# Sparse-attention softmax on negated scores with a running minimum, and a bisection step written as a one-tensor operation

## The chip, the cores and the metric

One Trainium2 chip, one core. The metric is the device time of one execution in microseconds (us), the median of the runs of a kernel. Engines: PE (matmul; PEld is its weight load), DVE (VectorE), ACT (ScalarE), POOL (GpSimd), SP (which issues most transfers).

## The reference

One layer of a streaming encoder over 1,056 rows: 1,024 of a prompt and 32 new rows of a running stream with 128 cached positions. What matters here:

```python
s = einsum('btnd,bld->btnl', qi, ki) * IDX_DIM**-0.5
score = einsum('btnl,btn->btl', relu(s), wi)          # 8 indexer heads
score = where(admissible, score, -inf)
_, idx = top_k(score, k_top)                          # 256 keys (40 for the running stream)
...
logits = einsum('btgrd,btkgd->btgrk', qg, k_sel) * HEAD_DIM**-0.5 + bias
p = softmax(where(valid, logits, NEG))
out = einsum('btgrk,btkgd->btgrd', p, v_sel)          # 8 heads of 64, 2 groups of keys
```

Around it stand one input projection, a gated convolution, the output projection, two layer norms and an MLP of width 4,096 with squared ReLU.

## The kernel before

Activations lie transposed (features on partitions). Products are done in three passes over high and low parts of the operands; the split into these parts is a copy on ACT (line L108) and a subtraction on POOL or DVE (L111). Up to the MLP a scheduler sets the order of the instructions of each engine when the kernel is built, from the program's order and its own estimates; from then on the order is that of the program. Each engine works through its own instructions strictly in the order so fixed.

**Choosing keys (`topk`, L423 on).** Queries are cut into tiles of 128 rows: tile t (0 to 7) sees (t+1)*128 keys; tile 8 is the running stream, with 160. No keys are gathered. For each row, 32 rounds of bisection on the bits of the score find the threshold that 256 keys exceed, and then ties are settled, so that the score tile becomes a mask (0 or a very negative number) which is added to the logits. Tiles 0 and 1 need no choice. A round counts the scores above the candidate, turns the count into a yes or no `v` (L448 or L450) and sets the next candidate `cand` from `v`, `cand` and a bit (L454). Tiles 7 and 6, and later 5, are bisected with `on_act=True`: ACT counts (L441), DVE does L448 and L454 on one element for each partition and tile. Tiles 2, 3, 4 and 8 are done together on DVE: L443 counts, and L450 and L454 handle four columns at a time. All this runs beside the projections, with their DVE evacuations L245, L246, L368, L388 and L414.

**Attention (`att_softmax`, `att_values`).** The tiles come in the order 7, 6, 8, 5, 4, 3, 2, 1, 0 (PLAN), each in four calls (g2 = 0 to 3) of two heads, with pieces of the output projection and of the first layer norm put in between. A call makes the logits on PE (L570 to L574) in one chunk of keys, or in two for tiles 4 to 7; one DVE instruction (L576) for each chunk adds the mask, writes the logits to SBUF and keeps their maximum. Then two small DVE instructions (L580, L581; for one chunk only L583) give the negated maximum `nm` of both heads, ACT takes the exponentials with it as bias and sums them (L586), DVE inverts the two sums (L588), and DVE and ACT scale one head each (L589, L590). PE transposes the weights (L608), ACT and DVE bring them to SBUF in two parts (L615, L616), and PE multiplies them with the values (L624, L625); L629 and L630 bring the result out.

Of the kernel before, what the change touches and what calls it, by code (L numbers as in the profile page):

```python
# [10 lines left out]
F32 = mybir.dt.float32  # L11
# [3 lines left out]
AF = mybir.ActivationFunctionType  # L15
OP = mybir.AluOpType
# [22 lines left out]
LOWEST = -(2.0 ** 126)  # L39
# [25 lines left out]
def f32(ap):  # L65
    return ap.bitcast(F32)
# [3 lines left out]
def hybrid_layer(ctx, tc, xT, win, wkw, wo, w1, w2, ckT, cv, ckiT, scT, cw, lnp, rb, cst, oh,  # L70
                 yT, kT_o, vT_o, kiT_o, pc_o, sc_o):
    nc = tc.nc
    V, S, G, PE = nc.vector, nc.scalar, nc.gpsimd, nc.tensor
# [5 lines left out]
    small = ctx.enter_context(tc.tile_pool(name="small", bufs=3))  # L79
# [20 lines left out]
    def qk_ps():  # L100
        return psum.tile([128, 512], F32, name="qk", bufs=4)

    def tr_ps():
        return psum.tile([128, 512], F32, name="tr", bufs=1)
# [152 lines left out]
    def key_chunks(N):  # L257
        c = (N + 511) // 512
        return [(i * (N // c), N // c) for i in range(c)]
# [34 lines left out]
    ps = tr_ps()  # L294
# [127 lines left out]
    def topk(ts, on_act):  # L422

        nb = len(ts)
        cand = small.tile([128, nb], I32, name="cand")
        cnt = small.tile([128, nb], F32, name="cnt")
        v = small.tile([128, nb], I32, name="v")
        dims = [(score[t], score[t].shape[0], score[t].shape[1], 256 if t < 8 else 40) for t in ts]
        V.memset(cnt, 0.0)

        def junk(R, N):
            return scr.tile([128, 768], F32, name="junka" if on_act else "junk").bitcast(BF16)[:R, :N]

        def scratch(R, n, name):
            return scr.tile([128, 768], F32, name=name)[:R, :n]

        for b in range(31, -1, -1):
            for i, (s, R, N, k) in enumerate(dims):
                c = 0.0 if b == 31 else f32(cand[:R, i:i + 1])
                if on_act:  # L440
                    S.activation(junk(R, N), s, AF.Sign, bias=c, scale=-1.0, accum_out=cnt[:R, i:i + 1])  # L441
                else:
                    V.tensor_scalar(junk(R, N), s, c, -float(k), op0=OP.is_ge, op1=OP.add, accum_out=cnt[:R, i:i + 1])  # L443
            w = -1.0 if b == 31 else float(1 << b)
            for i in (range(nb) if on_act else [slice(None)]):
                vi, ci, ni = (a[:, i:i + 1] if on_act else a for a in (v, cand, cnt))
                if on_act:
                    V.tensor_scalar(vi, ni, float(dims[i][2] - 2 * dims[i][3]), w, op0=OP.is_gt, op1=OP.mult)  # L448
                else:
                    V.tensor_scalar(vi, ni, 0.0, w, op0=OP.is_lt, op1=OP.mult)  # L450
                if b == 31:
                    V.tensor_scalar(ci, vi, 0x40000000, None, op0=OP.bitwise_xor)
                elif b:
                    V.scalar_tensor_tensor(ci, vi, 1 << (b - 1), ci, op0=OP.bitwise_xor, op1=OP.bitwise_xor)  # L454
                else:
                    V.tensor_tensor(ci, vi, ci, op=OP.bitwise_xor)
        if on_act:
            up = small.tile([128, 2, nb], F32, name="up", bufs=1)
            for i, (s, R, N, k) in enumerate(dims):
                th = f32(cand[:R, i:i + 1])  # L460
                V.tensor_scalar(junk(R, N), s, th, -float(k), op0=OP.is_gt, op1=OP.add, accum_out=cnt[:R, i:i + 1])
                for ci, (c, n) in enumerate(key_chunks(N)):
                    e = scratch(R, n, "tie")
                    V.tensor_scalar(e, s[:, c:c + n], th, BIG, op0=OP.is_le, op1=OP.mult)
                    V.tensor_tensor_reduce(e, e, s[:, c:c + n], 1.0, BIG, op0=OP.add, op1=OP.min,
                                           accum_out=up[:R, ci, i:i + 1])
            V.tensor_tensor(up[:, 0], up[:, 0], up[:, 1], op=OP.min)
            V.tensor_scalar(v, cnt, 0.0, -1.0, op0=OP.is_ge, op1=OP.mult)
            x = small.tile([128, nb], I32, name="x", bufs=1)
            V.tensor_tensor(x, cand, up[:, 0].bitcast(I32), op=OP.bitwise_xor)  # L470
            V.tensor_tensor(x, x, v, op=OP.bitwise_and)
            V.tensor_tensor(cand, x, cand, op=OP.bitwise_xor)
        for i, (s, R, N, k) in enumerate(dims):
            th = f32(cand[:R, i:i + 1])
            V.tensor_scalar(junk(R, N), s, th, -float(k), op0=OP.is_gt, op1=OP.add, accum_out=cnt[:R, i:i + 1])
            lim = small.tile([128, 1], F32, name="lim", bufs=1)
            V.tensor_scalar(lim[:R], cnt[:R, i:i + 1], -NEGP, None, op0=OP.mult)
            prev = 0.0
            for c, n in key_chunks(N):
                sc_ = s[:, c:c + n]  # L480
                e, rank = scratch(R, n, "tie"), scratch(R, n, "rank")
                V.tensor_scalar(e, sc_, th, NEGP, op0=OP.is_equal, op1=OP.mult)
                V.tensor_tensor_scan(rank, e, e, prev, op0=OP.add, op1=OP.bypass)
                if c + n < N:
                    carry = small.tile([128, 1], F32, name="carry", bufs=1)
                    V.tensor_copy(carry[:R], rank[:, n - 1:n])
                    prev = carry[:R]
                V.scalar_tensor_tensor(e, rank, lim[:R], e, op0=OP.is_lt, op1=OP.mult)
                V.tensor_scalar(sc_, sc_, th, NEGP, op0=OP.is_lt, op1=OP.mult)
                V.tensor_tensor(sc_, sc_, e, op=OP.add)  # L490

    topk((7, 6), True)
    topk((2, 3, 4, 8), False)
    proj_phase.close()

# [19 lines left out]
    def load_q(t, g):  # L515

        R = 128 if t < 8 else 32
        qs_[t, g] = pb.tile([128, 4, R], F32R, name="q", bufs=3)
        G.dma_start(qs_[t, g], qd[4 * g:4 * g + 4, :, t * 128:t * 128 + R].rearrange("h p t -> p h t"))
# [29 lines left out]
    def att_softmax(t, g2):  # L549

        R, N, k0 = (128, (t + 1) * 128, KP) if t < 8 else (32, 160, 0)
        if g2 % 2 == 0 and (t, g2 // 2) not in qs_:
            load_q(t, g2 // 2)
        q = qs_[t, g2 // 2]
        mask = edge[:R, 256 - N:256] if t < 2 else score[t]
        pad = 128 if t == 0 else 0
        g, h0 = g2 // 2, 2 * (g2 % 2)
        chunks = key_chunks(N)
        mx = small.tile([128, 2, 2], F32, name="mx")
        ls = []  # L560
        for i in range(2):
            L = pb.tile([128, 1024], F32, name="L", tag="L", bufs=LB)[:R, :N]
            ls.append(L)
            qh = q[:, h0 + i, :]
            for ci, (c, n) in enumerate(chunks):
                ps = qk_ps()
                last = ci == len(chunks) - 1
                w = max(n, 256)
                kc = slice(k0 + c - pad, k0 + c - pad + w)
                PE.matmul(ps[:R, :w], qh, kh[g][:, kc], start=True, stop=False)  # L570
                mm = PE.matmul(ps[:R, :w], qh, kl[g][:, kc], start=False, stop=not last)
                if last:
                    PE.matmul(ps[:R, w - 256:w], antir[:, :R], hh[g][:, h0 + i, :], start=False, stop=False)
                    mm = PE.matmul(ps[:R, w - 256:w], antir[:, :R], hl[g][:, h0 + i, :], start=False, stop=True)  # L574
                done["QK"] = mm
                V.tensor_tensor_reduce(L[:, c:c + n], ps[:R, pad:pad + n], mask[:, c:c + n], 1.0, LOWEST,  # L576
                                       op0=OP.add, op1=OP.max, accum_out=mx[:R, ci, i:i + 1])
        nm = small.tile([128, 2], F32, name="nm")
        if len(chunks) == 2:
            V.tensor_tensor(nm[:R], mx[:R, 0], mx[:R, 1], op=OP.max)  # L580
            V.tensor_scalar(nm[:R], nm[:R], -1.0, None, op0=OP.mult)  # L581
        else:
            V.tensor_scalar(nm[:R], mx[:R, 0], -1.0, None, op0=OP.mult)  # L583
        sm = small.tile([128, 2], F32, name="sm")
        for h in range(2):
            S.activation(ls[h], ls[h], AF.Exp, bias=nm[:R, h:h + 1], accum_out=sm[:R, h:h + 1])  # L586
        rs = small.tile([128, 2], F32, name="rs")
        V.reciprocal(rs[:R], sm[:R])  # L588
        V.tensor_scalar(ls[0], ls[0], rs[:R, 0:1], None, op0=OP.mult)  # L589
        S.activation(ls[1], ls[1], AF.Copy, scale=rs[:R, 1:2])  # L590
        return ls
# [736 lines left out]
    n = len(steps)  # L1328
# [124 lines left out]
```

## Time and profile before

| | us |
|---|---|
| median of 3 runs | 1344.34 (1343.89 to 1350.7) |
| the profiled execution's time | 1348.35 |
| its span, first to last instruction | 1346.6 |
| choosing keys beside the projections | about 109 to 362 of the span, tile 5 until 409 |
| attention | about 362 to 575 of the span |

Times are from one profiled execution. A matmul's record can overlap the next one's, so a busy PE isn't PE at its peak. A wait is put down to the instruction that released it.

### The profile page before, as it was taken

How to read it: one execution, taken by the hardware profiler on the slowest of the kernel's cores; microseconds unless marked ns; L12 is line 12 of the kernel's file. 1: busy time of each engine (PE TensorE's matmuls, PEld its weight loads, DVE VectorE, ACT ScalarE, POOL GpSimd, SP SyncE). 2: the span in 40 equal slices, each digit the busy share in tenths (PEclk: the TensorE clock that was granted, in tenths of full speed). 3: DMA queues.
4: the chain of work that ended last, by engine and by line, in shares of the span. 5: the costliest groups of instructions: out<-in, count | busy, mean ns of one | idle time of the engine just before them, and what ended most of it. 6: DMA issues, size and time to landing. Idle time of an engine off the chain costs nothing. (4 is left out here: it accounts for less than half of the span.)

```text
span 1346.6 us, 24097 instructions
## 1 busy us (share of the span) xinstructions
PE 1245.1 (92%) x8822; PEld 1203.5 (89%) x8822; DVE 994.9 (74%) x2043; ACT 692.8 (51%) x1378; POOL 564.6 (42%) x452
## 2 busy tenths in 40 slices
PE   7999999897899988896899999999999999998984
PEld 6999999897788987785899999999999999998884
DVE  5675899999488889878657667666557668586766
ACT  6666988644688878784322222222343444443323
POOL 2412344513521252363453553454445444447632
PEclk9999999899899998988899999999999999998987
DMA  6221111134531221243134343443863663542201
GB/s 209 92 68 37 48 33 47 48 108 152 166 87 18 47 65 32 71 141 122 45 108 150 138 153 139 147 154 137 302 234 91 196 187 113 176 144 87 65 33 65
DMA packets 97222, 149.98 MB, mean 111 GB/s; under 512 B 12456, under 2 KB 41808, under 8 KB 97104
## 3 DMA queue, kind: packets, MB, share of 16 engines
q1 hardware_dynamic: 81664, 139.55, 31.7%
q0 software_dynamic: 9504, 4.33, 1.9%
q10 hardware_dynamic: 5936, 4.58, 1.2%
q8 instruction: 69, 1.13, 0.4%
q14 instruction: 49, 0.40, 0.1%
HBM read 105.41 MB, written 43.00 MB: 110 GB/s over the span
## 5 line engine op out<-in xcount | busy, mean ns | idle before, releaser
L111 POOL TENSOR_TENSOR whl<-wraw,whl 128x512 fp32r<-128x512 f32 (+1 forms) x184 | 251.0, 1369 | 429.6 <-ACT whl L108 408.8
L858 PE MATMUL acc<-b,whl 128*128 128x264 f32 x1088 | 310.9, 286 | 6.1 <-DVE ring L937 3.0
L859 PE MATMUL acc<-b,whl 128*128 128x264 f32 x1088 | 310.7, 286 | 0.0
L860 PE MATMUL acc<-b,whl 128*128 128x264 f32 x1088 | 309.4, 284 | 0.0
L858 PEld LDWEIGHTS acc<-b,whl 128*128 128x128 f32 x1088 | 205.6, 189 | 7.1 <-DVE ring L937 3.2
L860 PEld LDWEIGHTS acc<-b,whl 128*128 128x128 f32 x1088 | 206.1, 189 | 0.0
L859 PEld LDWEIGHTS acc<-b,whl 128*128 128x128 f32 x1088 | 205.1, 189 | 0.1
L108 ACT ACTIVATE whl<-wraw 128x512 fp32r<-128x512 f32 (+1 forms) x184 | 113.1, 623 | 175.3 <-DVE wraw L853 143.2
L131 PE MATMUL mm<-xh,whl 128*128 128x384 f32 (+4 forms) x520 | 172.3, 332 | 14.3 <-ACT whl L108 5.6
L132 PE MATMUL mm<-area,whl 128*128 128x384 f32 (+4 forms) x552 | 182.9, 332 | 0.4 <-DVE area L111 0.4
L133 PE MATMUL mm<-xh,whl 128*128 128x384 f32 (+4 forms) x520 | 169.6, 331 | 0.0
L111 DVE TENSOR_TENSOR b<-xraw,b 128x528 fp32r<-128x528 f32 x94 | 69.7, 742 | 87.1 <-ACT b L108 87.0
L108 ACT ACTIVATE b<-xraw 128x528 fp32r<-128x528 f32 x94 | 60.5, 644 | 136.0 <-PE acc L860 82.1
L441 ACT ACTIVATE junka<-s,cand 128x1024 bf16<-128x1024 f32 (+1 forms) x93 | 96.5, 1037 | 42.0 <-DVE cand L454 34.2
L131 PEld LDWEIGHTS mm<-xh,whl 128*128 128x128 f32 (+1 forms) x520 | 97.9, 188 | 18.1 <-issue 8.1
L132 PEld LDWEIGHTS mm<-area,whl 128*128 128x128 f32 (+1 forms) x552 | 104.5, 189 | 2.9 <-DVE area L111 0.8
L133 PEld LDWEIGHTS mm<-xh,whl 128*128 128x128 f32 (+1 forms) x520 | 97.6, 188 | 3.2 <-POOL whl L111 1.2
L111 POOL TENSOR_TENSOR whl<-at,whl 128x512 fp32r<-128x512 f32 x56 | 81.5, 1465 | 30.8 <-ACT whl L108 30.8
L443 DVE TENSOR_SCALAR_CACHE_REDUCE junk<-s,cand 128x384 bf16<-128x384 f32 (+1 forms) x124 | 80.2, 647 | 1.3
L858 PE MATMUL acc<-area,whl 128*128 128x264 f32 x240 | 69.0, 288 | 0.0
L859 PE MATMUL acc<-area,whl 128*128 128x264 f32 x240 | 68.7, 286 | 0.0
L860 PE MATMUL acc<-area,whl 128*128 128x264 f32 x240 | 68.5, 286 | 0.0
(310 smaller groups left out, 3345.9 us busy)
## 6 DMA issues: line engine op xcount, KB each, us to landing
hd<-ring SPq DMA_DIRECT2D x98, 264.0 KB, 2.1
xraw<-hd SPq DMA_DIRECT2D x98, 264.0 KB, 2.7
at<-in_w_dram SPq DMA_DIRECT2D x58, 256.0 KB, 3.7
wraw<-in_win_dram SPq DMA_DIRECT2D x52, 256.0 KB, 2.6
wraw<-in_wo_dram SPq DMA_DIRECT2D x40, 256.0 KB, 2.7
w_a<-in_w_dram SPq DMA_DIRECT2D x23, 256.0 KB, 3.7
w_c<-in_w_dram SPq DMA_DIRECT2D x19, 256.0 KB, 3.4
zz<-zd SPq DMA_DIRECT2D x4, 1056.0 KB, 8.4
```

Source lines behind the costliest of these rows:

```text
L108: S.activation(hi, raw, AF.Copy)
L111: (lo_eng or G).tensor_tensor(lo, raw, f32(hi), op=OP.subtract)
L131: PE.matmul(ps, wh[k], a, start=(k == 0), stop=False)
L132: PE.matmul(ps, wh[k], b, start=False, stop=False)
L133: PE.matmul(ps, wl[k], a, start=False, stop=(k == K - 1))
L441: S.activation(junk(R, N), s, AF.Sign, bias=c, scale=-1.0, accum_out=cnt[:R, i:i + 1])
L443: V.tensor_scalar(junk(R, N), s, c, -float(k), op0=OP.is_ge, op1=OP.add, accum_out=cnt[:R, i:i + 1])
L858: PE.matmul(ps, wh, xhi, start=start, stop=False, skip_group_check=more)
L859: PE.matmul(ps, wh, xlo, start=False, stop=False, skip_group_check=more)
L860: PE.matmul(ps, wl, xhi, start=False, stop=stop, skip_group_check=more)
```

## The change

In `topk`, where ACT counts, the next candidate comes from a tensor-scalar instruction: `v` is then no second tensor but a scalar for each partition. The four-column form of the other tiles stays. In `att_softmax` the scores are written negated (the factor of L576 is -1) and their minimum is kept, so that it serves as the exponential's bias as it is, with a scale of -1 in the exponential. The joint steps L580, L581 and L583 go; for two chunks, a one-element minimum with a scalar for each partition stands before each head's exponential, and for one chunk nothing.

```diff
                 if b == 31:
                     V.tensor_scalar(ci, vi, 0x40000000, None, op0=OP.bitwise_xor)
+                elif b and on_act:
+                    V.tensor_scalar(ci, ci, vi, 1 << (b - 1), op0=OP.bitwise_xor, op1=OP.bitwise_xor)
                 elif b:
                     V.scalar_tensor_tensor(ci, vi, 1 << (b - 1), ci, op0=OP.bitwise_xor, op1=OP.bitwise_xor)
...
-        mx = small.tile([128, 2, 2], F32, name="mx")
+        mn = small.tile([128, 2, 2], F32, name="mn")
...
-                V.tensor_tensor_reduce(L[:, c:c + n], ps[:R, pad:pad + n], mask[:, c:c + n], 1.0, LOWEST,
-                                       op0=OP.add, op1=OP.max, accum_out=mx[:R, ci, i:i + 1])
-        nm = small.tile([128, 2], F32, name="nm")
-        if len(chunks) == 2:
-            V.tensor_tensor(nm[:R], mx[:R, 0], mx[:R, 1], op=OP.max)
-            V.tensor_scalar(nm[:R], nm[:R], -1.0, None, op0=OP.mult)
-        else:
-            V.tensor_scalar(nm[:R], mx[:R, 0], -1.0, None, op0=OP.mult)
+                V.tensor_tensor_reduce(L[:, c:c + n], ps[:R, pad:pad + n], mask[:, c:c + n], -1.0, -LOWEST,
+                                       op0=OP.add, op1=OP.min, accum_out=mn[:R, i, ci:ci + 1])
         sm = small.tile([128, 2], F32, name="sm")
         for h in range(2):
-            S.activation(ls[h], ls[h], AF.Exp, bias=nm[:R, h:h + 1], accum_out=sm[:R, h:h + 1])
+            if len(chunks) == 2:
+                V.tensor_scalar(mn[:R, h, 0:1], mn[:R, h, 0:1], mn[:R, h, 1:2], None, op0=OP.min)
+            S.activation(ls[h], ls[h], AF.Exp, bias=mn[:R, h, 0:1], scale=-1.0, accum_out=sm[:R, h:h + 1])
```

## Rows read from the trace of the kernel before

**Rows 1.** Busy time by stage; columns PE, PEld, DVE, ACT, POOL, granted clock, DMA.

```profile
139.00:250.00 111.00, 109.90 (x683) 109.24 (x681) 106.98 (x403) 100.00 (x201) 45.21 (x49) 1.00 0.14 42
250.00:362.00 112.00, 95.28 (x557) 91.75 (x557) 96.03 (x255) 54.20 (x109) 42.87 (x41) 0.95 0.43 129
362.00:562.00 200.00, 183.41 (x1203) 168.36 (x1204) 169.09 (x512) 159.06 (x356) 61.00 (x59) 0.96 0.22 53
```

**Rows 2.** What PE waited for, 250 to 365 us: total, times, longest.

```profile
PE mm L131 <- DVE qo L246: 7.5, 5, 2.8
PE mm L131 <- DVE y L388: 3.7, 1, 3.7
PE qk_b L570 <- DVE mx L576: 2.1, 1, 2.1
PE mm L131 <- DVE u L370: 1.6, 1, 1.6
```

**Rows 3.** What PE waited for, 365 to 565 us: total, times, longest.

```profile
PE qk_b L570 <- DVE mx L576: 4.6, 6, 2.2
PE tr_b L608 <- DVE pt L616: 4.3, 6, 1.3
PE pv_b L624 <- DVE ao L630: 3.1, 2, 2.7
```

**Rows 4.** Instructions of a line: duration in ns, min/median/max.

```profile
L448 DVE TENSOR_SCALAR v<-cnt x96: 131/148/155, 109.3 to 392.7; 128x1 int32<-128x1 f32 x96
L581 DVE TENSOR_SCALAR nm<-nm x16: 147/170/1997, 372.4 to 489.4; 128x2 f32<-128x2 f32 x16
```

**Rows 5.** DVE in order of time, at 361.7 and from 488 us: start, duration in us.

```profile
361.69 1.32 DVE L454 SCALAR_TENSOR_TENSOR cand<-v,cand 128x1 int32<-128x1 int32 x1
...
488.23 1.13 DVE L580 TENSOR_TENSOR nm<-mx 128x2 f32<-128x2 f32 x1
489.40 2.00 DVE L581 TENSOR_SCALAR nm<-nm 128x2 f32<-128x2 f32 x1
```

**Rows 6.** POOL in order of time, 487 to 492 us.

```profile
487.93 1.43 POOL L651 TENSOR_TENSOR junk<-junk,z 128x576 f32<-128x576 f32 x1
...
490.09 1.28 POOL L111 TENSOR_TENSOR whl<-wraw,whl 128x512 fp32r<-128x512 f32 x1
```

**Rows 7.** DVE groups by shape, 100 to 565 us: busy us, mean ns.

```profile
L454 DVE SCALAR_TENSOR_TENSOR cand<-v,cand 128x1 int32<-128x1 int32 x90 | 27.6, 307 | 0.6
...
L443 DVE TENSOR_SCALAR_CACHE_REDUCE junk<-s,cand 32x160 bf16<-32x160 f32 x31 | 11.2, 363 | 0.2
...
L580 DVE TENSOR_TENSOR nm<-mx 128x2 f32<-128x2 f32 x16 | 7.1, 446 | 0.2
...
L581 DVE TENSOR_SCALAR nm<-nm 128x2 f32<-128x2 f32 x16 | 5.5, 346 | 0.3
...
L583 DVE TENSOR_SCALAR nm<-mx 128x2 f32<-128x2 f32 x16 | 4.7, 291 | 0.2
...
L443 DVE TENSOR_SCALAR_CACHE_REDUCE junk<-s 32x160 bf16<-32x160 f32 x1 | 0.3, 307 | 0.0
```

**Rows 8.** The one-element L454 by stretch: 170:250, 271:328, 362:395 us.

```profile
L454 DVE SCALAR_TENSOR_TENSOR cand<-v,cand 128x1 int32<-128x1 int32 x42 | 12.3, 295 | 0.0
...
L454 DVE SCALAR_TENSOR_TENSOR cand<-v,cand 128x1 int32<-128x1 int32 x8 | 2.7, 335 | 0.0
...
L454 DVE SCALAR_TENSOR_TENSOR cand<-v,cand 128x1 int32<-128x1 int32 x8 | 5.1, 631 | 0.2
```

**Rows 9.** Waits of ACT and DVE in the softmax, 365 to 562 us.

```profile
ACT L L586 <- DVE nm L581: 8.0, 8, 2.6
...
ACT L L586 <- DVE nm L583: 3.4, 3, 1.5
...
DVE rs L588 <- ACT L L586: 17.5, 18, 2.9
```

**Rows 10.** PE after the stall of rows 5: start, duration, idle before.

```profile
492.05 1.25 PE L608 MATMUL tr_b<-cs,L 128*128 128x128 f32 x8 [1.05 <-DVE pt L616]
```

## Prediction

> **What bounds the kernel now.** I read the busy time by stage first [rows 1]. From 139 to 250 us PE has no gap to speak of (109.9 of 111), and DVE is as full (107.0). From 250 to 362 PE loses 16.7 us, from 362 to 562 another 16.6, while DVE is 86% and 85% busy. Then I asked what ended PE's idle time. Before 365 us it is DVE almost alone [rows 2]: evacuations of the projections (L245 and L246, L388, L368) that stand in DVE's queue behind bisection, and the first scores. In attention it is DVE again, 12.0 us in three rows [rows 3]. So in both stretches that the change touches, PE waits for DVE, and DVE time can be worth something. What follows attention is a chain of layer norm and MLP in a fixed order; I expect a shift there to pass to the end.
>
> The third view is how long the small DVE instructions take. One-element L448 takes 131 to 155 ns in all its 96 cases; two-element L581 takes 147 at least, 170 in the middle and up to 1997 [rows 4]. The long ones stand still beside POOL: L580 at 488.23 lasts 1.13 us and ends at 489.36, when POOL's L651 has just ended (489.36); L581 begins at 489.40 and ends at 491.40, when POOL's L111 has (491.37) [rows 5, 6]. The one-element L454 at 361.69 lasts 1.32 us [rows 5]; its 90 cases take 307 ns in the mean [rows 7]. The forms that suffer read two tensors (L454, L580) or are tensor-scalars of two elements (L581, L583). One-element tensor-scalars don't suffer, nor does L443, a tensor-scalar with a sum and with a scalar for each partition: 363 ns in the mean over 31 of 160 columns, against 307 for the one with a constant [rows 7].
>
> **The change part by part.** First the price of the new instruction, one element with a per-partition scalar; the trace has none. From below it is L448's 0.148 us [rows 4]. From above, with its stalls kept, it is L454's 0.307 [rows 7] plus what the scalar costs, 363 - 307 = 56 ns: 0.363. I take 0.148 + 0.056 = 0.204, near the lower end, since none of L448's 96 and of L443's 31 shows a stall although POOL is busy 41% of the time there (45.2 of 111).
>
> *Bisection.* 90 instructions go from 27.6 us to 90 x 0.204 = 18.4: DVE is freed of 9.2 us. What it is worth depends on the stretch [rows 8]:
> - 170 to 250: 42 x (0.295 - 0.204) = 3.8 us. PE has no gap here, so nothing comes back at once; but DVE is behind, and PE then waits 1.6 us for L368 and 3.7 us for L388, both at or shortly after 250 [rows 2]. DVE arrives 3.8 us earlier there, less than those 5.3. I count 3.8. If DVE only waits for PE instead, 0.
> - 271 to 328: 8 x (0.335 - 0.204) = 1.0 us, in the stretch where PE waits 7.5 us for L246. I count 1.0.
> - After 328 PE is full and tile 5's bisection, which is alone on its chain, isn't yet needed: its extra scalar read (about 56 ns a round) and its freed stalls are hidden. Should tile 5 be needed at once, 30 x 0.056 = 1.7 us would be owed.
> - At 362, L454's 1.32 us stands just before the first scores' L576, for which PE waits 2.1: 1.32 - 0.20 = 1.1 us. The other seven until 395 (5.1 us in all for eight) lie beside a full PE: 0.
>
> *Softmax.* L580, L581 and L583 with 128 rows cost 7.1 + 5.5 + 4.7 = 17.3 us [rows 7]. In their place stand 32 minima (16 calls with two chunks, two heads): 32 x 0.204 = 6.5. DVE gains 10.8 us. The pair at 488 goes from 3.13 us to 0.41; behind it PE waits 1.05 us at 492.05 [rows 10] and 2.2 for L576 soon after (the longest of its row [rows 3]). I count 2.7. Of the remaining 8.1 us I count a quarter, 2.0: DVE has 31 of 200 us free in this stage [rows 1], and the largest wait, 2.7 for L630, has other work before it. In this quarter lies what the earlier exponential gives: head 0 no longer waits for head 1's scores and the joint steps. ACT's wait for these is 11.4 us and DVE's wait for the exponentials 17.5 [rows 9], so the chain does get shorter, but ACT has only 41 of 200 us free and works its queue in order.
>
> *What costs nothing.* L576 with a factor of -1 and a minimum is the same instruction over the same columns; the exponential had a bias for each partition already, and its scale is a constant. No transfer and no buffer of size is added.
>
> *Sum.* 3.8 + 1.0 + 1.1 + 2.7 + 2.0 = 10.6 us. Some stalls will be handed on: a later DVE instruction meets the same POOL instruction. Behind the cases I looked at stand mostly L443, L576 and L616, which don't stall, so I take off 1 us: 9.6. From the profiled execution's 1348.35 that gives 1338.8. That execution lay 4.0 above the median, so for the median I take 1344.34 - 9.6, about 1335.
>
> **The rivals.**
>
> *The freed DVE time is hidden.* For it: from 139 to 250 PE is full, and each evacuation in DVE's queue ties DVE to PE's pace; in attention DVE already waits 17.5 us for ACT. Then only the pieces next to a PE gap count, 1.1 + 2.7 less the 1 handed on, and the time is 1344.3 - 2.8 = 1341.5. Against it: PE's gaps from 250 on all end with DVE.
>
> *The new instruction stalls as the old did.* Then bisection costs 90 x 0.056 = 5 us more DVE time, of which those of the first two stretches of [rows 8] reach PE, 50 x 0.056 = 2.8, and the softmax saves 17.3 - 32 x 0.363 = 5.7 us, of which the share above, 4.7 of 10.8, counts: 2.5. Sum: +0.3, or 1344.6. The Trainium skill names a rule by which this could happen: the page "SBUF — State Buffer", section "Who interferes with whom", has tensor-scalars in a two-port mode block against GpSimd, and "VectorE: DVE Perf Modes" (section "What auto-detection actually checks") lets an operation into that mode when the outermost dimensions are even or equal, which one element against one element could be read to satisfy. By that rule L448 would stall too; the trace has none in 96, so I give it little.
>
> *Slower: ACT's queue.* Each exponential now has a wait of its own. If the scheduler puts head 0's exponential early, ACT can stand in front of it, or of head 1's, while transposed weights (L615) wait behind it, and PE behind those. Price: a wait as today's mean, 11.4 / 11 = 1.0 us, in each of 36 calls is 36 us against the 41 that ACT has free. It decides once ACT's added waits pass those 41 us, or fall where PE waits for L615; then I put it at a quarter of 36, +9 us: 1353. Against it: today's ACT waits are few (11 in 72 exponentials). The same loss could come from another order of DVE's evacuations, since the scheduler orders everything up to the MLP anew.
>
> **How the numbers follow.** The forecast has 0.58, the hidden gain 0.26, the new stall 0.06, slower 0.10. The prediction is the forecast's, 1335. Its own range is 1326 (all of DVE's 9.2 + 10.8 us, short of 2, comes back) to 1340 (half the sum). The whole range reaches down to 1322, where waits of the earlier exponential come back as well, and up to 1346, to take in the hidden gain and the new stall; the slower case stays outside with a little at the low end. Half a per cent, 6.7 us, is what a measurement of this kernel can tell from no change. Faster by more means below 1337.6: most of the forecast, 0.55. Within: the rest of it with the two middle rivals, 0.34. Slower: 0.11.
>
> **What would show it.** Right: no DVE instruction of one element above some 0.25 us at L454's place and at the minima; the group of 90 at about 18 us; DVE's busy time down by some 20; the PE waits for L388, L368 and, around 490, for L616 and L576 smaller; the start of attention about 5 us earlier and its end about 10; the MLP stage as long as before. Wrong: minima of 1 us and more beside POOL (the second rival); the 90 short but attention starting at the same time (the first); ACT idle before L586 well above 11.4 us with PE waiting for L615 (the third). A changed order of instructions beside all this would make the sum wrong in size without making the mechanism wrong.

## The result, and the profile after

The changed kernel takes 1325.85 us (median of 5 runs, 1324.16 to 1326.95); the kernel before, run beside it, took 1349.29 (5 runs, 1343.89 to 1350.7). The ratio is 0.9836, 95% interval 0.9818 to 0.9854: 22 us (19.6 to 24.5) faster. (The table ahead of the prediction has 1344.34 for the kernel before, a median of three of these runs.) The forecast was 1335, its range 1322 to 1346: right in direction and inside the range, but the sum of 9.6 us is less than half of what came. The profiled execution has a span of 1325.2 us against 1346.6.

In the tables below, "attention starts" is the start of the first scores' matmul and "attention ends" the end of the last L624 (L622 after the change; the L625 behind it ends 0.2 us later), both read from the traces. From before to after they go from 360.2 and 575.1 to 349.5 and 555.3: 10.7 us come before attention, 9.1 in it, and what follows adds only 1.6. Up to the end of attention PE's idle time falls by 13 us (48.4 to 35.3); the other 7 us are busy time, 527.0 us before and 520.2 after for the same matmuls.

Busy time by stage of the changed kernel, as in [rows 1]:

```profile
139.00:250.00 111.00, 111.00 (x692) 110.92 (x692) 105.36 (x411) 101.19 (x206) 48.40 (x51) 1.00 0.15 44
250.00:362.00 112.00, 100.78 (x589) 96.71 (x588) 93.29 (x263) 57.64 (x112) 45.57 (x42) 0.95 0.46 140
362.00:562.00 200.00, 183.46 (x1218) 170.06 (x1217) 166.60 (x496) 168.19 (x378) 62.42 (x60) 0.96 0.22 53
```

DVE is busy for 105.36, 93.29 and 166.60 us, 1.6 to 2.7 less than before in each stage, though more work has passed (692 and 589 matmuls in the first two stages against 683 and 557); PE's one idle microsecond before 250 us is gone, and in the second stage PE idles 11.2 us instead of 16.7. What PE waited for, 250 to 365 us, as in [rows 2]:

```profile
PE mm L131 <- DVE qo L246: 5.7, 5, 1.9
PE mm_b L131 <- DVE v L448: 1.9, 1, 1.9
PE qk_b L572 <- DMA q<-qd: 1.2, 1, 1.2
PE mm L131 <- DVE z L414: 1.0, 1, 1.0
```

and 365 to 565 us, as in [rows 3]:

```profile
PE pv_b L622 <- DVE ao L628: 5.6, 3, 3.7
PE qk_b L572 <- DVE mn L578: 5.0, 5, 2.5
...
PE tr_b L606 <- DVE pt L614: 1.2, 3, 0.5
```

(Lines below the edit have moved: before's L576 is L578 here, L586 is L584, L589 is L587, L616 is L614, L630 is L628.) The waits for L388 (3.7 us) and L370 (1.6) are gone, that for L616 has fallen from 4.3 to 1.2. That for the output evacuation seems to have grown, from 3.1 to 5.6, but the stretch of [rows 3] ends before the last two of these waits in the kernel before, which has from 562 us on:

```profile
PE pv_b L624 <- DVE ao L630: 5.3, 2, 3.7
```

Over the whole of attention it falls from 8.4 to 5.6 us, and that for the scores from 6.7 to 5.3. The new instructions by shape, 100 to 565 us, as in [rows 7]:

```profile
L454 DVE TENSOR_SCALAR cand<-cand,v 128x1 int32<-128x1 int32 x90 | 18.6, 207 | 0.6
L583 DVE TENSOR_SCALAR mn<-mn 128x1 f32<-128x1 f32 x32 | 6.6, 207 | 0.3
```

Both cost 207 ns in the mean; the forecast took 204. No one of them stalls (the row of durations of L583 stands with the second group of experiments).

### The profile page after: what moved, and what is told of

Read it like the earlier page. It is cut to its first block, busy times and chain, and to the rows that moved or that the text cites. A ratio compares the mean times of both kernels' runs of the same rounds, so it can differ in the third digit from the quotient of the medians.

```text
span 1325.2 us, 24062 instructions
## 1 busy us (share of the span) xinstructions
PE 1237.5 (93%) x8822; PEld 1199.8 (91%) x8822; DVE 976.5 (74%) x2023; ACT 692.7 (52%) x1378; POOL 565.5 (43%) x452
## 5 line engine op out<-in xcount | busy, mean ns | idle before, releaser
L111 POOL TENSOR_TENSOR whl<-wraw,whl 128x512 fp32r<-128x512 f32 (+1 forms) x184 | 251.7, 1373 | 413.1 <-ACT whl L108 394.1
L111 DVE TENSOR_TENSOR b<-xraw,b 128x528 fp32r<-128x528 f32 x94 | 69.8, 742 | 86.4 <-ACT b L108 86.2
L111 POOL TENSOR_TENSOR whl<-at,whl 128x512 fp32r<-128x512 f32 x56 | 81.0, 1457 | 30.7 <-ACT whl L108 30.7
```

The source lines that it names most:

```text
L111: (lo_eng or G).tensor_tensor(lo, raw, f32(hi), op=OP.subtract)
```

## The experiments

All ratios are to the kernel before, run on the same chip in turn. One per cent is 13.5 us. The changed instructions also changed the order that the scheduler wrote for every engine, so most experiments hold an order: from a list, each instruction of an engine gets an edge (issue order only, no wait) from the one that is to stand ahead of it, up to the MLP.

```diff
-    qs = [plain(0), plain(1), plain(2), last_quarter()]
+    qs = [plain(0), plain(1), plain(2), last_quarter()]; hold_order(tc, nc)
```

| kernel | ratio, 95% interval | us against before | attention starts, ends (profile) |
|---|---|---|---|
| changed | 0.9836, 0.9818 to 0.9854 | -22 | 349.5, 555.3 |
| e1: bisection's part alone | 0.9909, 0.9888 to 0.9930 | -12 | 349.6, 563.8 |
| e2: softmax's part alone | 0.9925, 0.9905 to 0.9944 | -10 | 359.9, 568.5 |
| h1: new step, before's order | 0.9940, 0.9920 to 0.9960 | -8 | 353.0, 564.5 |
| h2: old step, order of e1 | 0.9954, 0.9936 to 0.9971 | -6 | 352.8, 565.9 |
| h3: changed, old step | 0.9855, 0.9829 to 0.9880 | -20 | 353.4, 558.7 |
| h4: changed, two-tensor minima | 0.9843, 0.9818 to 0.9868 | -21 | 349.4, 555.0 |
| h5: changed, both | 0.9873, 0.9849 to 0.9897 | -17 | 352.7, 559.4 |
| h6: changed, joint exponentials | 0.9874, 0.9849 to 0.9899 | -17 | 348.7, 556.7 |
| h7: old instructions, new order | 0.9978, 0.9964 to 0.9993 | -3 | 351.5, 572.5 |
| h8: new instructions, old order | 0.9898, 0.9877 to 0.9919 | -14 | 352.9, 561.0 |
| h9: before, one evacuation moved | 0.9990, 0.9977 to 1.0003 | -1 | 359.0, 574.2 |
| h10: changed, eight moves on DVE | 0.9856, 0.9834 to 0.9878 | -19 | 348.5, 552.7 |

**First group: the parts, and instruction against order.** e1 has only the step in `topk`, e2 only the softmax, each with the order that the scheduler made for it. h1 is e1's instructions in before's order, h2 before's instructions in e1's order.

```diff
+                elif b and on_act:
+                    V.tensor_scalar(ci, ci, vi, 1 << (b - 1), op0=OP.bitwise_xor, op1=OP.bitwise_xor)
```

> Only the bisection's one-element step is changed; the softmax is that of before. If the two parts add up as the two traces suggest (attention starts 10.7 us earlier in the changed kernel, and ends 19.8 earlier), this one is about 11 us faster than before and attention starts about 11 earlier. By the sum of the prediction it would be 5.9 faster (3.8 + 1.0 + 1.1). If the softmax alone made the gain, it is within 3 us of before.

> Only the softmax is changed (negated scores, running minimum, one-element minima); the bisection keeps the two-tensor step. If the parts add up, about 9 us faster than before, with attention starting where it did before and lasting 9 us less. By the prediction's sum 4.7 faster. If the bisection alone made the gain, within 3 us of before.

> The bisection's step is changed as in the run of the bisection alone, but every engine is made to issue its instructions up to the MLP in the order of the kernel before; so only the instruction's own time differs. Theory of the stalls: DVE waits no longer for POOL at this step, its 90 cases take some 18.6 us instead of 27.6, and the time falls by 5 to 8 us. Rival, the new order is what gains: within 2 us of before, and the gain stands in the next run instead.

> The reverse: the bisection's step is the two-tensor one of before, with the issue order of the run with the bisection alone. Theory of the stalls: within 3 us of before, with some 20 stalls of about 0.6 us at this step. Rival, the new order is what gains: 5 us or more faster than before with the stalls still there.

The parts add: 12 + 10 us are the whole change's 22. For the step, the new instruction alone is worth 8 us (h1) and the new order alone 6 (h2), together 12; that they overlap by 2 is within what the intervals leave open. In h1, with not one instruction at another place, attention starts 7.2 us earlier and gets 3.4 us shorter (211.5 against 214.9).

**Second group: the old forms in the changed kernel's order.** h3 puts the scalar-tensor-tensor step back, h4 writes the minima with two tensors, h5 does both. h6 changes no instruction, only where head 0's minimum and exponential stand.

```diff
-                V.tensor_scalar(mn[:R, h, 0:1], mn[:R, h, 0:1], mn[:R, h, 1:2], None, op0=OP.min)
+                V.tensor_tensor(mn[:R, h, 0:1], mn[:R, h, 0:1], mn[:R, h, 1:2], op=OP.min)
```

> The changed kernel with its own issue order held on every engine up to the MLP, and only the bisection step put back to the old scalar-tensor-tensor form (90 instructions, same values). If the freed stalls of the step are worth the same beside the new softmax as they were in the old order (about 8 us there, 6 in the order of the bisection change alone), the time rises from 1325.9 by 6 to 8, to about 1333. Rival: the two parts overlap, and with the softmax lighter the step is worth at most 3 us: 1329 or less.

> The changed kernel with its own issue order held, and only the 32 one-element minima written as tensor-tensor (two tensors read) instead of a per-partition scalar. If they stall beside GpSimd as the joint maximum did (0.446 us in the mean against 0.207 now), DVE gets 32 x 0.24 = 7.7 us more, and about half of it, 4 us, reaches the end: 1330. Rival: where these minima now stand they seldom meet a GpSimd instruction, or what they lose is hidden: no more than 1 us, under 1327.

> The changed kernel, its own issue order held, with both old forms put back: the scalar-tensor-tensor step and the tensor-tensor minima. If the two stalls add, this is the sum of the other two runs, some 10 to 12 us above the changed kernel: 1337. What is then left to the kernel before (1346.9 to 1349.3), about 10 us, isn't stalls of these instructions but the order, the 16 instructions that went and the earlier exponential. Rival: the stalls are the whole change, and this comes within 3 us of the kernel before.

> The changed kernel with not one instruction changed; its own issue order is held but for one thing: in each call of the attention head 0's minimum is issued just behind head 1's and head 0's exponential just before head 1's, so that head 0 waits for head 1's scores as it did before the change. If the earlier exponential is worth much, the attention takes 3 to 6 us longer: 1329 to 1332, with more idle time of ACT before the exponentials and of PE before the transposes. Rival: ACT and DVE have other work to put there, and the time stays within 1.5 us of 1325.9.

h3 and h4 went the rivals' way: by the ratios they are 2.6 and 1 us above the changed kernel, and their intervals overlap its own; only h5, at 5 us, nearly stands apart. The step's form, worth 8 us in the old order, measures 2.6 in the new one (uncertain by some 4), although it frees nearly as much DVE time there (h3's 90 take 26.1 us against 18.6); the profile of h3 has attention start 3.9 us later. The minima, durations in ns (min/median/max) in the changed kernel and then in h4:

```profile
L583 DVE TENSOR_SCALAR mn<-mn x32: 185/208/216, 359.7 to 472.7; 128x1 f32<-128x1 f32 x32
```

```profile
L583 DVE TENSOR_TENSOR mn<-mn x32: 129/156/2450, 357.6 to 472.3; 128x1 f32<-128x1 f32 x32
```

The two-tensor form is quicker at the median by 52 ns and has stalls up to 2.45 us; over 32 it costs 9.1 against 6.6 us, and the time doesn't show it (1 us, uncertain by some 4).

h6 is 5 us above the changed kernel, with intervals that just overlap. In the profile attention lasts 208.0 us against 205.8. A two-chunk call in each trace shows what is lost. The changed kernel, DVE in order of time (start, duration in us):

```profile
364.67 0.68 DVE L578 CUSTOM_DVE_ANT_0 L<-qk_b,s 128x512 f32<-128x512 f32 x1
...
365.37 0.69 DVE L578 CUSTOM_DVE_ANT_0 L<-qk_b,s 128x512 f32<-128x512 f32 x1
...
366.11 0.21 DVE L583 TENSOR_SCALAR mn<-mn 128x1 f32<-128x1 f32 x1
...
368.94 0.69 DVE L578 CUSTOM_DVE_ANT_0 L<-qk_b,s 128x512 f32<-128x512 f32 x1
...
369.67 0.21 DVE L583 TENSOR_SCALAR mn<-mn 128x1 f32<-128x1 f32 x1
```

and ACT:

```profile
367.29 1.14 ACT L584 ACTIVATE L<-L,mn 128x1024 f32<-128x1024 f32 x1
```

In h6 DVE, in a call of the same shape:

```profile
363.51 0.68 DVE L578 CUSTOM_DVE_ANT_0 L<-qk_b,s 128x512 f32<-128x512 f32 x1
364.23 0.33 DVE L583 TENSOR_SCALAR mn<-mn 128x1 f32<-128x1 f32 x2
```

and ACT:

```profile
364.60 1.15 ACT L584 ACTIVATE L<-L,mn 128x1024 f32<-128x1024 f32 x1 [1.22 <-DVE mn L583]
365.75 1.13 ACT L584 ACTIVATE L<-L,mn 128x1024 f32<-128x1024 f32 x1
```

In the changed kernel head 0's exponential is over at 368.43, before head 1's last scores begin at 368.94. In h6 both minima stand together, ACT has idled 1.22 us, and the two exponentials follow each other.

**Third group: the whole square, and single places.** h7 has all old instructions in the changed kernel's order, h8 all new ones in before's order; the exponentials of a call stand together in both. h9 moves one instruction of the kernel before, h10 eight places of the changed one; both hold all other issue order.

> All instructions of the kernel before, issued on every engine up to the MLP in the order of the changed kernel; only the two exponentials of a call stand together, as they must behind the joint maximum. If the new order is a large part of the gain, this is well below the kernel before: the two old forms cost the changed kernel 5 us and the joined exponentials another 5, and the 20 more instructions some 2, which makes 1326 + 12 = 1338, or 10 below the kernel before. Rival: the order only pays once the instructions are short, and the time is that of the kernel before, 1346 or more.

> All instructions of the changed kernel, issued on every engine up to the MLP in the order of the kernel before, the exponentials of a call together again. This is what the forecast's sum priced: 9.6 us below the kernel before, about 1338. The bisection step alone gave 8 us in the old order, so that with the softmax's 3 to 5 us it should be 1335 to 1337. Rival: the instructions alone make the whole gain and the order is by the way: 1326 to 1328.

> The kernel before, no instruction changed, its issue order held but for one: the first evacuation of the convolution (it ran at 261.10 us) is issued ahead of the tie work, at about 256.9. If the order's worth lies in such places, PE's wait of 3.7 us before 261.8 goes and with it the stretch at the low clock behind it (6 us at 0.58, 2.5 us lost), so that the attention starts 4 to 6 us earlier and the time falls by as much, to 1343. Rival: another evacuation or wait takes its place, and the time stays within 1.5 us of the kernel before.

> The changed kernel, no instruction changed, its issue order held but for eight places on DVE: five pairs of query evacuations, a pair of evacuations of the gate's product, two score evacuations with a scaling at 498 us and one output evacuation at 552 us go in front of the bisection, tie or layer norm work that stood ahead of them (0.5 to 3.5 us each). PE waits 5.8 us for the first six and 6.2 for the last two. If DVE's order is what is left to gain, the time falls by 5 to 8 us, to 1318 to 1321. Rival: the work put back is late in its turn, or PE then waits for the next evacuation: 1324 or more.

| | before's order | changed kernel's order |
|---|---|---|
| old instructions | 0 | -3 (h7) |
| new instructions | -14 (h8) | -22 |

The instructions alone are 14 us (10.9 to 16.6). The order alone is 3, and 8 on top of the new instructions. But the 8 holds more than places: old instructions, and h8, have the two exponentials of a call together, and the changed kernel hasn't. With them together and the new instructions the new order is worth 3 as well (h8's -14 to h6's -17), and 5 come with the separate exponentials. These steps of 3 and 5 are each uncertain by some 4. In h7 attention starts 8.7 us earlier and then takes 6.1 longer (221.0 against 214.9), so that little is left.

h9 shows what becomes of one instruction moved by itself. PE in the kernel before:

```profile
261.79 0.66 PE L131 MATMUL mm<-xh,whl 128*128 128x384 f32 x1 [3.67 <-DVE y L388]
```

and DVE there:

```profile
256.89 0.14 DVE L456 TENSOR_TENSOR cand<-v,cand 128x1 int32<-128x1 int32 x1
...
257.47 1.23 DVE L454 SCALAR_TENSOR_TENSOR cand<-v,cand 128x4 int32<-128x4 int32 x1
```

PE, DVE and POOL in h9:

```profile
263.32 0.52 PE L131 MATMUL mm<-xh,whl 128*128 128x384 f32 x1 [2.72 <-DVE y L388]
```

```profile
256.88 0.54 DVE L388 TENSOR_TENSOR y<-mm,y 128x384 f32<-128x384 f32 x1
257.35 1.26 DVE L456 TENSOR_TENSOR cand<-v,cand 128x1 int32<-128x1 int32 x1
...
258.64 1.21 DVE L464 TENSOR_SCALAR tie<-s,cand 128x512 f32<-128x512 f32 x1
259.77 0.15 DVE L454 SCALAR_TENSOR_TENSOR cand<-v,cand 128x4 int32<-128x4 int32 x1
...
264.90 1.78 DVE L465 CUSTOM_DVE_ANT_0 tie<-tie,s 128x512 f32<-128x512 f32 x1
```

```profile
257.31 1.29 POOL L111 TENSOR_TENSOR whl<-wraw,whl 128x512 fp32r<-128x512 f32 x1 [1.37 <-ACT whl L108]
258.55 1.01 POOL L111 TENSOR_TENSOR cl<-y,ch 128x384 fp32r<-128x384 f32 x1
```

The moved L388 runs at 256.88 instead of 261.10. But the L456 behind it, 0.14 us at 256.89 in the kernel before, now stands beside POOL's L111 and takes 1.26 us, while the four-column L454 that stood there goes from 1.23 to 0.15: that stall has changed hands. The L464 between them goes from 0.48 to 1.21, and the second L465 from 0.68 to 1.78. PE waits 2.72 us for the second L388 where it waited 3.67 for the first, and the last L388 ends at 267.1 instead of 265.2.

h10 was to be a faster kernel, and the times don't show one: its ratio is above the changed one's, and the intervals overlap. Ahead of attention PE's wait for L246 falls from 5.7 to 4.6 us, and one for L414 grows from 1.0 to 2.2. At the end of attention PE in the changed kernel:

```profile
552.32 0.54 PE L622 MATMUL pv_b<-pt,vv 128*128 128x256 f32 x1 [3.73 <-DVE ao L628]
554.71 0.58 PE L622 MATMUL pv_b<-pt,vv 128*128 128x256 f32 x1 [1.63 <-DVE ao L628]
```

PE and DVE in h10:

```profile
546.23 0.38 PE L622 MATMUL pv_b<-pt,vv 128*128 128x256 f32 x1 [0.92 <-DVE ao L628]
552.08 0.58 PE L622 MATMUL pv_b<-pt,vv 128*128 128x256 f32 x1 [5.34 <-DVE ao L628]
```

```profile
545.76 0.42 DVE L628 TENSOR_TENSOR ao<-pv_b,ao 64x256 f32<-64x256 f32 x1 [1.64 <-ACT ao L627]
546.10 3.53 DVE L660 TENSOR_TENSOR z<-z,st_b 128x768 f32<-128x768 f32 x4
549.56 0.94 DVE L666 TENSOR_TENSOR junka<-junka,tie 128x768 f32<-128x768 f32 x1
```

L628 now stands ahead of the four L660, DVE stands idle 1.64 us for ACT before it, and the next L628 is late by the 3.5 us that were put back: 3.73 + 1.63 = 5.36 us of waits have become 0.92 + 5.34 = 6.26. In this place the wait went to the next evacuation.

## Why the prediction was right, and where it was short

**The mechanism and the price were right.** L454's 90 fell from 27.6 to 18.6 us, 9.0 where 9.2 were forecast. The joint steps' 17.3 us became 6.6, 10.7 where 10.8 were. The new instruction costs 207 ns against 204, and none of the 122 is above 217 ns beside POOL, so the rival with the kept stalls (1344.6) is out. The Trainium skill, "SBUF — State Buffer", section "Who interferes with whom", has a DVE instruction with two SBUF inputs contend with a GpSimd instruction that reads SBUF, and one with a single input, outside the two-port modes, not: the traces agree for the minima (216 ns at most in the changed kernel, against 2450 with two inputs in h4).

**Stalls handed on: 1 us was of the right size.** With four joint steps of 32 rows (0.8 us), which the sum left out, 20.5 us were freed. DVE's busy time fell by 18.4 us over the whole span (994.9 to 976.5), so some 2 came back. The scaling L587 alone went from 18.3 to 22.8 us; others got shorter.

**The term that was too small is the step's.** The sum gave it 5.9 us (3.8, 1.0 and 1.1); h1, with the order held, measured 8 us (5.4 to 10.8), and in its profile attention ends 10.6 earlier. As no instruction of h1 has changed places, every matmul can be set beside the same one of the kernel before, and how much earlier it starts shows where the gain arises:

| matmul | start before | start in h1 | earlier by |
|---|---|---|---|
| ahead of the waits for L370 and L388 | 247.01 | 246.85 | 0.2 |
| behind them | 261.79 | 255.98 | 5.8 |
| a little later | 267.59 | 259.27 | 8.3 |
| behind the last wait for L246, at L414 | 325.04 | 318.20 | 6.8 |
| first scores | 360.23 | 353.02 | 7.2 |
| behind the first waits for scores and `v` | 365.25 | 357.55 | 7.7 |
| a little later | 369.25 | 359.74 | 9.5 |
| at 394 us | 393.98 | 384.55 | 9.4 |
| at 478 us | 478.54 | 467.93 | 10.6 |
| end of attention | 574.52 | 563.96 | 10.6 |

*Around 250 to 262.* The sum counted 3.8 of the 5.3 us of waits; both are gone, since the first L388 runs 6.2 us earlier (254.93 instead of 261.10). (The row of the 1.6 us names L370, not L368 as in the prediction.) Then 2.5 us more come without any wait, over these matmuls, in the kernel before and in h1 (columns as in [rows 1]):

```profile
262.00:268.00 6.00, 6.00 (x22) 6.00 (x23) 6.00 (x19) 1.69 (x4) 4.47 (x4) 0.58 0.14 44
```

```profile
256.00:259.40 3.40, 3.40 (x22) 3.40 (x21) 3.40 (x7) 1.09 (x3) 3.18 (x4) 1.00 0.27 82
```

In the kernel before PE had stood idle for 3.67 us, and the granted clock was 0.58 in the mean of the next 6 us, most of that at the lower of its two levels (0.50, or 1.2 GHz); some 22 matmuls took 6.0 us. In h1 PE didn't stand idle there, the clock was 1.00, and as many took 3.4.

*From 271 to 328* the sum counted 1.0, out of the wait for L246. That wait is 7.5 us in the kernel before and 7.3 in h1:

```profile
PE mm L131 <- DVE qo L246: 7.3, 7, 2.1
```

PE comes into this stretch 8.3 us earlier and leaves it 6.8 earlier: 1.5 are lost again.

*At the first scores* the sum counted 1.1. Their wait falls from 2.13 to 0.55 us, but the one behind it, for `v` of L448, grows from 0.35 to 1.94. So the waits together are no shorter. What is gained are 1.8 us in the twelve matmuls that follow (4.0 us before, 2.2 in h1), again at the two levels of the clock:

```profile
362.60:369.40 6.80, 5.38 (x15) 4.66 (x16) 2.32 (x8) 3.03 (x6) 4.04 (x3) 0.50 0.28 90
```

```profile
355.40:362.20 6.80, 4.52 (x24) 4.01 (x24) 3.09 (x11) 3.60 (x8) 4.93 (x3) 1.00 0.40 120
```

*The seven instructions after 362* were put at nothing. They gave nothing by 394 us (9.5 at 369, 9.4 at 394) and at most the 1.2 that come later, in small pieces at 404 and from 475 to 479. In the whole of attention PE is idle for 23.8 us in both kernels; the 3.4 us by which h1's attention is shorter are, net, busy time:

```profile
360.20:575.30 215.10, 191.29 (x1236) 174.05 (x1236) 180.26 (x530) 168.38 (x374) 66.31 (x62) 0.95 0.23 57
```

```profile
353.00:564.80 211.80, 187.98 (x1236) 171.80 (x1236) 176.68 (x530) 167.65 (x374) 66.40 (x62) 0.97 0.24 59
```

So the sum priced a wait by its length, and put at nothing that the matmuls behind it ran at the lower clock: 2.5 and 1.8 us in these two places. This comes from one execution of each kernel. The clock differs between executions (its mean over the span is 0.964 to 0.973 in 23 runs of the kernel before, 0.968 in the mean of 15 beside h1 and 0.970 in h1's six), so how much of the 8 us is due to it in every run isn't shown.

**The softmax's term was of the right size by the profile.** The sum counted 4.7 of 10.8 us, less the 1 handed on. From h1 to h8 attention ends 3.5 us earlier, and 3.7 of these come between 444 and 500 us of h1's span, around the pair for which the sum had 2.7. By the times it is 14 - 8 = 6 us, uncertain by some 4. So in the old order the forecast's 9.6 stands against 14 (10.9 to 16.6). By the profiles the missing 4 are the step's; the times can't tell.

**The rest, 8 us, is the new order with the separate exponentials, which the sum left out.** The prediction named a changed order as what would make the sum wrong in size. The separate exponentials need the new order, and h6 gives them 5 us by the times (2.2 by the profile); the sum had them inside a quarter of 8.1 us, 2.0 for all of it. The remaining 3 us are the places of other instructions. Which ones isn't settled: h9 and h10 moved nine and gained nothing that can be measured, and the intervals of the held kernels are each 3.5 to 7 us wide. That the time lies inside the whole range is luck in part: at 1325.85 it is just below the forecast's own range (1326 to 1340), and it came that low by what the sum left out.

**The rivals.** *Hidden gain* (1341.5): out, since h8 alone is below it. *ACT's queue* (1353): ACT's waits for scores and minima are 9.6 us against 11.4 for the joint steps, DVE's wait for the exponentials fell from 17.5 to 3.2, and PE's for the transposed weights from 4.3 to 1.2; so the price didn't come. But the waits that it feared are there in small. ACT now waits 6.4 us (nine times) for the inverted sums, against 1.0 before, and DVE 6.7 instead of 0.2 for ACT's half of the transposed weights; PE loses 1.8 us, once, to a late scaling on ACT. All that PE waits for at the transposes falls from 5.8 to 4.3. The waits of ACT in the changed kernel, 350 to 550 us, as in [rows 9]:

```profile
ACT L L584 <- DVE mn L578: 6.8, 10, 1.6
...
ACT L L584 <- DVE mn L583: 2.8, 3, 1.9
```

and of DVE:

```profile
DVE rs L586 <- ACT L L584: 3.2, 5, 1.2
```

Of the signs named, the 90 at 18 us came (18.6), DVE's fall by some 20 (18.4), the shorter PE waits at L388, L370 and L616, and the MLP stage as long as before (its accumulation 654.0 and 652.5 us). Attention's start and end, forecast about 5 and 10 us earlier, came 10.7 and 19.8 earlier, twice the size.

## What to carry to other kernels

When a wait of PE is to go, look also at the clock of the matmuls behind it: in two places here they gave 2.5 and 1.8 us on top. DVE time that was freed beside a full PE counted where a wait of PE for DVE followed (at 250 and 262 us), and little where none did (after 362). A change of instructions also changes the order of a scheduler that plans with them; hold the order in one run and the instructions in another, and the two parts of the gain come apart. With the order held, compare the start of each matmul in both kernels: the gain arises where the difference grows. Moving single instructions forward in a full queue can hand the wait to the next one, as h9 and h10 did.

## What the runs showed of the hardware that was not expected

A scalar for each partition costs a one-element DVE instruction 52 ns at the median (208 against 156 with two tensors), so the form that can stall is the cheaper one where it meets no stall. Over h4's 32 minima the stalls add 9.1 - 32 x 0.156 = 4.1 us, one of them 2.3, and 1 us, uncertain by some 4, is seen in the time.

Behind a wait of 3.67 us PE's granted clock was 0.58 for 6 us, and the matmuls there took 2.5 us longer than where that wait was gone: two thirds of the wait once more.
